# Other PSUM banks and another last quarter product for the seventh product of a two-level Winograd matmul

## The chip, the cores and the metric

The kernel runs on one core of one Trainium2 chip. The time is the device time of one execution in microseconds; the number compared is the median over runs.

## The reference

Two fp32 matrices of 4096 x 4096 are multiplied and a leaky ReLU with slope 0.01 follows.

```python
x = np.matmul(a, b)                       # 4096 x 4096 by 4096 x 4096, fp32
return np.where(x > 0, x, alpha * x)      # alpha = 0.01
```

## The kernel before

**Regions.** The output is cut into sixteen regions of 1024 x 1024: four groups `g` (1024 rows each) by four columns `j`. The first region is done in a plain way; the other fifteen stand in the list `regions`, three of group 0 and then four of each of the groups 1, 2 and 3. Matrices are rounded to fp16 on their way in; products add up in fp32 in the eight PSUM banks (128 x 512 each).

**One region.** A region is one step of the Strassen-Winograd scheme: seven products of 512 x 2048 by 2048 x 512 in place of eight. A product, made by `product` (line 722), is 64 matmuls of 128x128 by 128x512 into four banks. The four banks of one set are called `y`, those of the other `z`; from region to region the sets change places (`ybank`, `zbank`), so the next region's first product writes the four banks that are `z` now, `zbank + 0` first, then `+1`, `+2`, `+3`. Sums of A's blocks (`sum_a`, line 531) and of B's blocks (`b_sum`, line 561) are made on VectorE; results are collected in fp32 tiles `c` by ScalarE copies (`keep`, line 735) and VectorE adds (`add`, line 815). `leave` applies the leaky ReLU (line 307) and stores (line 820).

**Quarters.** In nine regions the scheme is applied a second time to the seventh product, and in six of these (`both`) to the sixth too; the three others are the first regions of the groups 1 to 3. Then the product is seven quarter products (`quarter_product`, line 673) of 16 matmuls of 128x128 by 128x256 each. `into(bank)` lets the result lie in one extra bank; `onto(r, n)` lets it add to what two of the banks `y` hold already. In the names of the code `x[h, k]` are quarters of the A operand, `b[k, n]` quarters of the B operand, `sx(1)` to `sx(4)` the four sums of A quarters, `t(1)`, `t(2)`, `t(4)` the sums of B quarters. The A sums of one group do not change, so they are made once (`sums_of_a`, line 657, in the group's first region), kept in DRAM (line 658) and loaded again in the two later regions by `load_sums` (line 667). `following(n)` inside `sixth_in_quarters` issues the load of sum `n` for the seventh product; the room that it loads into holds a sum of the sixth product, and the load waits until that sum's quarter product is done: sum 4 waits for `sx1 t1`, sum 2 for `sx2 t2`, sum 1 for `sx4 b11`, sum 3 for `sx3 b01`.

**Order.** The order of the work on each engine is written out by hand: every engine executes its instructions in the order of the code. The DMAs of line 667, the stores of line 820 and the loads of `load_s2` (line 692) are issued by one queue (SP) in that order; the loads of B (`fetch_unit`, line 505) by another (POOL).

**Rooms.** Three pools matter: three rooms `a16` (512 KB each, fp16 128 x 2048), three rooms `x` (2 MB each) and the PSUM banks. A room is written again when its last reader is done; a store to DRAM is such a reader. The tile `t` with the name `q` is one room `x` cut into four parts `t[:, 0]` to `t[:, 3]`; it holds the B sums `tq` and one A sum.

**The two places.** In the six regions `sixth_in_quarters` makes its quarter products in the order `x00 b00`, `sx1 t1`, `x01 b10`, `sx2 t2`, `sx4 b11`, `x11 t4`, `sx3 b01`, in the banks `one, other, third, fourth` (`zbank + 0` to `+ 3`); then comes `seventh_in_quarters`, called as

```python
kept_c = seventh_in_quarters(y, new_bank(zbank + 3), new_bank(zbank + 1), tq, sq)
```

Its order is `x01 b10`, `x00 b00`, `sx4 b11`, `x11 t4`, `sx2 t2`, `sx1 t1`, `sx3 b01`. Its bank `one` is taken up by ScalarE copies at lines 798, 802 and 807 (twice, from the last state of `one`), its bank `other` by VectorE adds at lines 804 and 808, where 808 adds to what a copy of line 807 has made. After it the next region begins.

Of the kernel before, what the change touches and what calls it, by code (L numbers as in the profile page):

```python
# [46 lines left out]
def kernel(  # L47
# [40 lines left out]
    x = small_pool.tile([P, 8], FP32, name="x")  # L88
# [99 lines left out]
    def load_b(j, u, c, wide, nt):  # L188
        nc.gpsimd.dma_start(new_b(j, u, nt)[:, c:c + wide, :], b_rows(j, u, c, wide, nt))
# [13 lines left out]
    def new_bank(i):  # L203
        return psum_pool.tile([P, NT], FP32, name="ps", tag=f"ps{i}")
# [88 lines left out]
    for i, (_, h, u, _, _) in enumerate(steps):  # L293
        made = pieces_a(0, h, u, i == 1) if i else []
        more = []
        if u not in seen:
            more = [lambda u=u, c=c, nt=nt: load_b(0, u, c, 2, nt)
                    for c in range(0, KC, 2) for nt in range(2)]
# [47 lines left out]
    both = []  # L346
# [98 lines left out]
    for i in range(1, len(steps)):  # L445
        t, h, u, first, last = steps[i]
# [16 lines left out]
        t, h, u, first, last = steps[i]  # L463
# [161 lines left out]
    def b_quarter(t):  # L625
        return t.rearrange("p (c n) -> p c n", n=HALF)
# [12 lines left out]
    def sums_of_b(y, to, some=(2, 4, 1)):  # L639
        tt = nc.vector.tensor_tensor  # L640
        f = lambda n: b_quarter(to[n])
        if 2 in some:
            tt(f(2), y[0, 1], y[0, 0], ADD)
        if 4 in some:
            tt(f(4), y[1, 0], f(2), SUB)
        if 1 in some:
            tt(f(1), y[1, 1], f(2), SUB)

    def sums_of_a(g, name, room):

        x = {key: q.rearrange("p c m e -> p c (m e)") for key, q in quarters_of_a(g, name).items()}
        made = {}

        def make(n, x0, x1, op):
            made[n] = room(n)
            f = lambda t: made[t].rearrange("p (c m) -> p c m", m=2 * HALF) if isinstance(t, int) else x[t]
            nc.vector.tensor_tensor(f(n), f(x0), f(x1), op)
            nc.sync.dma_start(kept_q[name][n - 1], made[n])

        make(1, (1, 0), (1, 1), ADD)  # L660
        make(2, 1, (0, 0), SUB)
        make(3, (0, 0), (1, 0), SUB)
        make(4, (0, 1), 2, SUB)
# [5 lines left out]
    def quarter_product(xq, yq, to, first=False):  # L669
        for c in range(KC):  # L670
            for m in range(2):
                rows = slice(m * P, (m + 1) * P)
                nc.tensor.matmul(  # L673
                    to[m], xq[:, c // 2, rows, c % 2], yq[:, c, :],
                    start=first and (c, m) == (0, 0), stop=c == KC - 1, skip_group_check=True,
                )

    def into(bank):
        return [bank[:, m * HALF:(m + 1) * HALF] for m in range(2)]

    def pair(bank):
        return bank.rearrange("p (m n) -> p m n", m=2)

    def new_a16(_=None):
        return a16_pool.tile([P, QUARTER], DT, name="q16", tag="a16")
# [18 lines left out]
    for i, (g, j) in enumerate(regions):  # L704
# [7 lines left out]
        zbank = 4 - ybank  # L712
# [25 lines left out]
        def sixth_in_quarters(pairs, banks, v, y, tq, sq):  # L738


            b = quarters_of_b(i, 1, 0)
            x = quarters_of_a(g, "a22")
            one, other, third, fourth = banks
            t = lambda n: b_quarter(tq[n])
            sx = lambda n: a_quarter(sq[n])
            next_t, next_s = {}, {}
            y7 = quarters_of_b(i, 1, 1)

            def more(r, n, t):
                block = pairs[r][:, :, n * HALF:(n + 1) * HALF]  # L750
                nc.vector.tensor_add(block, pair(t), block)

            def following(n, room=None):
                next_s[n] = new_a16() if room is None else room
                load_sums("s4", next_s, (n,))

            quarter_product(x[0, 0], b[0, 0], into(one), True)
            add(v[:2], y[:2])
            more(0, 0, one)
            add(v[2:], y[2:])  # L760
            quarter_product(sx(1), t(1), into(other), True)
            more(1, 1, other)
            following(4)
            next_t[2] = tq[1]
            quarter_product(x[0, 1], b[1, 0], into(fourth), True)
            leave(v, 1, 1)
            quarter_product(sx(2), t(2), into(one))
            following(2)
            more(0, 1, one)
            sums_of_b(y7, next_t, (2,))  # L770
            more(0, 0, fourth)
            quarter_product(sx(4), b[1, 1], into(other))
            following(1, sq[4])
            next_t[4] = tq[2]
            sums_of_b(y7, next_t, (4,))
            more(0, 1, other)
            quarter_product(x[1, 1], t(4), into(third), True)
            next_t[1] = tq[4]
            sums_of_b(y7, next_t, (1,))
            more(1, 0, third)  # L780
            quarter_product(sx(3), b[0, 1], into(one))
            following(3)
            more(1, 0, one)
            more(1, 1, one)
            return next_t, next_s

        def seventh_in_quarters(y, one, other, tq, sq):

            pairs, kept = new_c(side)
            b = quarters_of_b(i, 1, 1)  # L790
            x = quarters_of_a(g, "s4")
            t = lambda n: b_quarter(tq[n])
            sx = lambda n: a_quarter(sq[n])
            block = lambda r, n: pairs[r][:, :, n * HALF:(n + 1) * HALF]
            onto = lambda r, n: [y[2 * r + m][:, n * HALF:(n + 1) * HALF] for m in range(2)]
            quarter_product(x[0, 1], b[1, 0], onto(0, 0))
            quarter_product(x[0, 0], b[0, 0], into(one), True)
            nc.scalar.copy(block(0, 0), pair(one))  # L798
            quarter_product(sx(4), b[1, 1], onto(0, 1))
            quarter_product(x[1, 1], t(4), onto(1, 0))  # L800
            quarter_product(sx(2), t(2), into(one))
            nc.scalar.copy(block(0, 1), pair(one))
            quarter_product(sx(1), t(1), into(other), True)
            nc.vector.tensor_add(block(0, 1), pair(other), block(0, 1))  # L804
            quarter_product(sx(3), b[0, 1], into(one))
            for n in (1, 0):
                nc.scalar.copy(block(1, n), pair(one))
            nc.vector.tensor_add(block(1, 1), pair(other), block(1, 1))  # L808
            for mt in range(MT):
                nc.vector.tensor_add(kept[mt], y[mt], kept[mt])  # L810
            return kept
# [29 lines left out]
        y = [new_bank(ybank + mt) for mt in range(MT)]  # L841
# [4 lines left out]
        first_of_group = i == 0 or regions[i - 1][0] != g  # L846
        in_quarters = g > 0 and not turning and not final
        both = in_quarters and not first_of_group
# [40 lines left out]
            sum_a(g, "s4")  # L889
        if late_ones:  # L890
            late_ones[0].end()
        if first_of_group and g:
            sums_of_a(g, "a22", new_a16)
        if in_quarters:
            t = x_pool.tile([P, 4, QUARTER], DT, name="q", tag="x")
            tq, sq = {2: t[:, 0], 1: t[:, 1], 4: t[:, 2]}, {4: t[:, 3]}
        if both:
            for n in (1, 2, 3):
                sq[n] = new_a16()
            load_sums("a22", sq, (1, 2, 3, 4))  # L900
# [22 lines left out]
        if turning:  # L923
            new_s(g + 1, "s1")
            t = new_s(g + 1, "s2").rearrange("p k c m e -> p (k c m e)").bitcast(BF16)
            a21 = measure(i + 1, 0, 1, 0, t.rearrange("p (n w) -> p n w", n=4))
            a21.begin()
        if both:
            tq, sq = sixth_in_quarters(u2_pairs, [new_bank(zbank + mt) for mt in range(MT)], v, y, tq, sq)
# [26 lines left out]
                sum_a(g + 1, name)  # L956

        if in_quarters:
            kept_c = seventh_in_quarters(y, new_bank(zbank + 3), new_bank(zbank + 1), tq, sq)
            fetch_b(i + 1, [(1, 1)], (1, 0))  # L960
            new_s(g, "s2")
            load_s2(g, 1)
            leave(kept_c, 0, 1)
        else:
            product(6, y, False)
            fetch_b(i + 1, [(1, 1)], ks)
            if final:
                even = nc.values_load(good[0:1, 0:1], min_val=0, max_val=1)
            _, kept_c = new_c(side)

            def store(mt):
                nc.sync.dma_start(place(g, 0, mt, j, 1), kept_c[mt])

            for mt in range(MT):
                nc.scalar.copy(kept_c[mt], y[mt])  # L975
                leaky(kept_c[mt])
                if not (final and mt == MT - 1):
                    store(mt)
# [5 lines left out]
    with inputs.Else():  # L984
        for m in range(M // RM):
            a_blocks = []
            for u in range(KU):
                t = a_pool.tile([P, KC // 2, RM, 2], BF16, name="a", tag=f"a{u // 2 + 1}{m % 2 + 1}")
# [6 lines left out]
            for n in range(N // NT):  # L995
                banks = [new_bank(n % 2 * 4 + mt) for mt in range(MT)]
                cols = slice(n * NT, (n + 1) * NT)
                for u in range(KU):
                    t = b_pool.tile([P, KC, NT], BF16, name="b", tag=f"b{u // 2 + 1}{n % 2 + 1}")
# [8 lines left out]
                for mt in range(MT):  # L1008
                    t = c_pool.tile([P, 2, NT], FP32, name="c", tag=f"c{side}")[:, 0]
# [38 lines left out]
```

## Time and profile before

| | us |
|---|---|
| three runs | 1573.12, 1574.47 (median), 1579.82 |
| the profiled execution, its own time | 1580.19 |
| its span, first to last instruction | 1578.3 |
| TensorE (PE) busy | 1549.3 (98%) |
| VectorE (DVE) busy | 1127.2 (71%) |
| ScalarE (ACT) busy | 373.3 (24%) |
| GpSimd (POOL) busy | 299.6 (19%) |
| mean granted TensorE clock | 0.998 |

Times in the views of the trace count from the span's first instruction. PE is the matmul unit, PEld its weight load; SPq marks an issue of the SP queue. In a row of the timeline the columns are the start, the duration, the engine, line and operation, what it writes and reads, the count, and in brackets the idle time of the engine before it with what ended that. A matmul's duration includes its way through the array, so one row of 16 overlaps the next; the distance between starts is what it costs.

### The profile page before, as it was taken

The numbers are of one execution on the slowest core, as the hardware profiler recorded it, in microseconds if no ns is written. First come the engines' busy times: TensorE is split into PE (matmuls) and PEld (weight loads), VectorE is DVE, ScalarE is ACT, GpSimd is POOL, SyncE is SP. The second block draws the span as 40 slices with busy tenths as digits, with TensorE's granted clock in tenths as the row PEclk, the third lists the DMA queues.
The fourth block names the chain that finished last, engine by engine and source line by source line (L and its number), as shares of the span: only waits on it lengthen the run. The fifth ranks groups of instructions, "written<-read, shape, count | busy, mean of one in ns | idle before, by whom it ended". The sixth has DMA issues, their size and how long they took to land. (4 is left out here: it accounts for less than half of the span.)

```text
span 1578.3 us, 20106 instructions
## 1 busy us (share of the span) xinstructions
PE 1549.3 (98%) x7995; PEld 781.1 (49%) x7995; DVE 1127.2 (71%) x1265; ACT 373.3 (24%) x390; POOL 299.6 (19%) x482
## 2 busy tenths in 40 slices
PE   9999999999999999999999999999999989999997
PEld 4444444444445455474444547456444454745543
DVE  4378758777975776956797686784879779587463
ACT  2201243512111314301211340511122143151230
POOL 5641110244002011123401102012430110201100
PEclk9999999999999999999999999999999999999999
DMA  9999795999739699599976939789995892969902
GB/s 242 183 214 187 154 279 148 193 200 193 273 87 268 153 191 263 128 265 207 194 274 157 266 95 264 179 179 276 190 251 198 187 266 86 261 162 193 260 27 83
DMA packets 206057, 310.76 MB, mean 197 GB/s; under 512 B 18049, under 2 KB 155521, under 8 KB 199042
## 3 DMA queue, kind: packets, MB, share of 16 engines
q0 software_dynamic: 149376, 141.59, 56.2%
q1 hardware_dynamic: 56290, 167.41, 28.6%
q8 instruction: 64, 1.05, 0.3%
q10 hardware_dynamic: 288, 0.39, 0.1%
q14 instruction: 39, 0.32, 0.1%
HBM read 354.42 MB, written 94.37 MB: 284 GB/s over the span
## 5 line engine op out<-in xcount | busy, mean ns | idle before, releaser
L722 PE MATMUL ps<-b,a 128*128 128x512 f16 x3456 | 754.3, 379 | 11.3 <-DVE c L808 10.7
L722 PEld LDWEIGHTS <-a 128*128 128x128 f16 x3456 | 337.3, 98 | 420.0 <-DVE c L808 14.2
L722 PE MATMUL ps<-b,s 128*128 128x512 f16 x2304 | 503.2, 379 | 0.0
L722 PEld LDWEIGHTS <-s 128*128 128x128 f16 x2304 | 225.5, 98 | 271.8
L561 DVE TENSOR_TENSOR b<-b 128x4096 f16<-128x4096 f16 x112 | 252.7, 2288 | 95.2 <-DMA b<-in_b_dram 83.5
L505 POOL DMA_DIRECT2D b<-in_b_dram x184 | 136.3, 746 | 948.2 <-PE ps L722 625.4
L735 ACT COPY c<-ps 128x512 f32<-128x512 f32 x180 | 92.3, 598 | 484.3 <-PE ps L722 422.7
L139 DVE STREAM_TRANSPOSE a<-a 128x512 uint32<-128x512 uint32 (+2 forms) x120 | 126.7, 1102 | 86.1 <-DMA a<-in_a_dram 84.2
L130 POOL DMA_DIRECT2D a<-in_a_dram x252 | 137.4, 552 | 200.3 <-DVE a L139 118.4
L307 DVE SCALAR_TENSOR_TENSOR c<-c 128x512 f32<-128x512 f32 x240 | 149.4, 684 | 12.7 <-ACT c L975 10.0
L815 DVE TENSOR_TENSOR c<-ps,c 128x512 f32<-128x512 f32 x156 | 97.0, 681 | 85.7 <-PE ps L722 59.2
L227 ACT ACTIVATE sq<-b 128x2048 bf16<-128x2048 f16 x64 | 119.2, 1909 | 107.1 <-DVE sq L236 82.7
L279 PE MATMUL ps<-b,a 128*128 128x512 f16 x512 | 113.0, 379 | 2.8 <-DMA b<-in_b_dram 1.4
L227 ACT ACTIVATE sq<-a 128x2048 bf16<-128x2048 f16 x48 | 89.0, 1910 | 88.7 <-DVE sq L236 67.9
L673 PEld LDWEIGHTS <-q 128*128 128x128 f16 x960 | 94.1, 98 | 11.1
L279 PEld LDWEIGHTS <-a 128*128 128x128 f16 x512 | 49.7, 98 | 63.9 <-issue 3.4
L798 ACT COPY c<-ps 128x512 f32<-128x512 f32 x9 | 5.3, 586 | 263.8 <-PE ps L673 263.8
L673 PE MATMUL ps<-b,q 128*128 128x256 f16 x480 | 57.5, 273 | 0.0
L673 PEld LDWEIGHTS <-s 128*128 128x128 f16 x432 | 43.0, 99 | 10.8 <-issue 4.7
L804 DVE TENSOR_TENSOR c<-ps,c 128x512 f32<-128x512 f32 x9 | 6.2, 691 | 58.1 <-issue 49.8
L239 DVE TENSOR_TENSOR sq<-sq 128x2048 bf16<-128x2048 bf16 x27 | 33.1, 1225 | 17.4 <-ACT sq L227 17.4
L673 PE MATMUL ps<-q,q 128*128 128x256 f16 x384 | 45.4, 273 | 0.0
(94 smaller groups left out, 718.0 us busy)
## 6 DMA issues: line engine op xcount, KB each, us to landing
b<-in_b_dram POOLq DMA_DIRECT2D x192, 512.0 KB, 13.5
out_dram<-c SPq DMA_DIRECT2D x240, 256.0 KB, 6.1
a<-in_a_dram POOLq DMA_DIRECT2D x244, 128.0 KB, 5.5
b<-kept SPq DMA_DIRECT2D x24, 1024.0 KB, 8.2
s<-kept_s SPq DMA_DIRECT2D x18, 1024.0 KB, 7.4
q<-kept_qa SPq DMA_DIRECT2D x24, 512.0 KB, 6.8
q<-kept_qs SPq DMA_DIRECT2D x24, 512.0 KB, 8.8
b<-in_b_dram POOLq DMA_DIRECT2D x24, 256.0 KB, 9.3
```

Of the source, the lines that this page charges most:

```text
L130: nc.gpsimd.dma_start(a16[32 * q:32 * q + 32], src.rearrange("(g i) w -> i g w", i=32))
L139: nc.vector.transpose(part.rearrange("p c m e -> p c (m e)").bitcast(U32) .rearrange("p c (g i) -> p g c i", i=32), src[:, :, i * n:(i + 1 ...
L227: nc.scalar.activation(to, self.parts[n], SQUARE)
L239: nc.vector.tensor_add(total, total, self.held[3])
L279: nc.tensor.matmul(ps, a_cols(at[0, h, u], c, mt, (h, u) == (0, 0)), bt[0, u, nt][:, c, :], start=first, stop=last,)
L307: nc.vector.scalar_tensor_tensor(t, t, alpha, t, op0=MULT, op1=MAX if alpha <= 1 else MIN)
L505: nc.gpsimd.dma_start(t[:, c:c + 4, :], b_rows(j, u, c, 4, nt, g > 0))
L561: nc.vector.tensor_tensor(f(to), f(x0), f(x1), op)
L673: nc.tensor.matmul(to[m], xq[:, c // 2, rows, c % 2], yq[:, c, :], start=first and (c, m) == (0, 0), stop=c == KC - 1, skip_group_check=True,)
L722: nc.tensor.matmul(banks[mt], a_cols(t, c, mt, t is first_a), B(half, nt, k)[:, c, :], start=first and (k, c) == todo[0], stop=(k, c) == t ...
L735: nc.scalar.copy(kept[mt], banks[mt])
L815: nc.vector.tensor_add(to, bank, to)
```

## The change

1. `seventh_in_quarters` gets other extra banks: `one` is `zbank + 3` in the six regions as before and `zbank + 0` in the three; `other` is `zbank + 2` in all nine.
2. In `seventh_in_quarters` the quarter product `x11 t4`, which adds to the banks `y[2]` and `y[3]`, moves from the fourth place to the last, behind the copies and adds that empty `one` and `other`.
3. In `sixth_in_quarters` (the six regions) the quarter products `x11 t4` and `sx3 b01` change places, and with them the VectorE work and the load of sum 3 that follow each.
4. In the three first regions the tile `t` is made before the A sums of `a22`; the sums 2, 3 and 4 are written into `t[:, 0]`, `t[:, 1]`, `t[:, 2]` and only sum 1 into a room `a16`. Before, all four went through the three rooms `a16`.

```diff
             more(0, 1, other)
-            quarter_product(x[1, 1], t(4), into(third), True)
-            next_t[1] = tq[4]
-            sums_of_b(y7, next_t, (1,))
-            more(1, 0, third)
             quarter_product(sx(3), b[0, 1], into(one))
             following(3)
             more(1, 0, one)
             more(1, 1, one)
+            quarter_product(x[1, 1], t(4), into(third), True)
+            more(1, 0, third)
+            next_t[1] = tq[4]
+            sums_of_b(y7, next_t, (1,))
             return next_t, next_s
...
             quarter_product(sx(4), b[1, 1], onto(0, 1))
-            quarter_product(x[1, 1], t(4), onto(1, 0))
             quarter_product(sx(2), t(2), into(one))
...
             nc.vector.tensor_add(block(1, 1), pair(other), block(1, 1))
+            quarter_product(x[1, 1], t(4), onto(1, 0))
             for mt in range(MT):
...
-        if first_of_group and g:
-            sums_of_a(g, "a22", new_a16)
         if in_quarters:
             t = x_pool.tile([P, 4, QUARTER], DT, name="q", tag="x")
             tq, sq = {2: t[:, 0], 1: t[:, 1], 4: t[:, 2]}, {4: t[:, 3]}
+        if first_of_group and g:
+            sums_of_a(g, "a22", lambda n: new_a16() if n == 1 else t[:, n - 2])
...
-            kept_c = seventh_in_quarters(y, new_bank(zbank + 3), new_bank(zbank + 1), tq, sq)
+            kept_c = seventh_in_quarters(y, new_bank(zbank + (3 if both else 0)), new_bank(zbank + 2), tq, sq)
```

## The prediction

> **What bounds the kernel now.** I read the page's busy times first, then the waits of PE, then the timeline at each place where PE waited. The page:
>
> ```profile
> PE 1549.3 (98%) x7995; PEld 781.1 (49%) x7995; DVE 1127.2 (71%) x1265; ACT 373.3 (24%) x390; POOL 299.6 (19%) x482
> ```
>
> PE is the bound: of the span of 1578.3 us it is idle for 29.0. An edit that leaves the count of matmuls alone can win only what PE waits, and loses whatever it makes PE wait. The waits of PE (us in total, times, longest) have two rows that touch the change:
>
> ```profile
> PE ps L722 <- DVE c L808: 10.7, 9, 1.2
> PE ps L673 <- DVE c L815: 4.1, 3, 3.8
> ```
>
> The first occurs once in each of the nine quartered regions, at the start of the next region. The timeline around the end of one of them:
>
> ```profile
> 604.43 0.38 PE L722 MATMUL ps<-b,a 128*128 128x512 f16 x1
> 604.63 1.07 ACT L807 COPY c<-ps 128x512 f32<-128x512 f32 x2 [2.91 <-DMA out_dram<-c]
> ...
> 605.25 0.69 DVE L808 TENSOR_TENSOR c<-ps,c 128x512 f32<-128x512 f32 x1 [1.62 <-ACT c L807]
> ...
> 606.00 0.39 PE L722 MATMUL ps<-b,a 128*128 128x512 f16 x1 [1.19 <-DVE c L808]
> ```
>
> At 604.43 the last quarter product is through, the next region gets one matmul into `zbank + 0`, and the second matmul, into `zbank + 1` = `other`, waits 1.19 us for copy and add of lines 807 and 808.
>
> The second row is two waits of under 0.2 us and one of 3.8 us, in the first region of group 3. There VectorE is late, because the A sums share three rooms whose stores must land first (the indented row is what ended line 657's idle time in that region: 7.4 us, four times):
>
> ```profile
> 1241.18 1.22 DVE L657 TENSOR_TENSOR q<-a,a 128x2048 f16<-128x2048 f16 x1
> ...
> 1262.93 2.48 DVE L815 TENSOR_TENSOR c<-ps,c 128x512 f32<-128x512 f32 x4
> ...
> 1267.73 2.48 DVE L815 TENSOR_TENSOR c<-ps,c 128x512 f32<-128x512 f32 x4
> ```
>
> ```profile
>   DMA kept_qa<-q: 7.4, 4
> ```
>
> ```profile
> 1264.58 1.91 PE L673 MATMUL ps<-b,s 128*128 128x256 f16 x16
> 1270.27 3.41 PE L673 MATMUL ps<-b,s 128*128 128x256 f16 x16 [3.78 <-DVE c L815]
> 1273.47 2.12 PE L673 MATMUL ps<-b,q 128*128 128x256 f16 x16
> 1275.42 1.91 PE L673 MATMUL ps<-q,s 128*128 128x256 f16 x16
> ```
>
> ```profile
> 1270.00:1274.00 4.00, 3.73 (x19) 2.70 (x19) 2.62 (x5) 0.29 (x1) 0.00 (x0) 0.57 1.15 285
> ```
>
> The seventh product's second quarter goes into `zbank + 3`, the last bank that the adds at 1267.73 empty. The wait costs more than itself: in the window behind it (the column 0.57 is the granted clock) the two quarters take 3.20 and 1.95 us from start to start, 1.66 us above twice 1.745. Its whole price is 3.78 + 1.66 = 5.4 us. Behind the nine waits of 1.19 us the clock does not fall.
>
> **The banks and the last quarter product.** After the change the region ends with `x11 t4` into `y[2]`, `y[3]`, which the next region does not need for two products. The copy and the add run under it: with `sx3 b01` ending at time E, the rows above put the copy at E + 0.20 to 1.27 and the add at E + 0.82 to 1.51. A quarter product takes 1.745 us from start to start (rows at 683.60 to 687.09 below), so PE comes to the first of these banks at E + 1.74 at the earliest: 0.23 us or more to spare at `other`, 0.47 or more at `one`. So all nine waits go: **-10.7**. In the three first regions `one` is the bank that the adds of line 815 empty first; the 0.3 us of small waits goes too. The two ScalarE copies have 1.74 us of PE work between a product into `one` and the next into it (lines 798 and 802; the first had twice that), against 0.2 us and half of the 1.07 us that two copies take: no wait.
>
> **The A sums of the first regions.** Without the room waits the twelve VectorE steps from 1241.18 (four `a22` sums, four `s4` sums, four of B, 1.2 us each) end near 1255.7. Two waits can remain: the third `s4` sum takes the room of the first `a22` sum, and the B sums take `t[:, 0]` to `t[:, 2]`, whose stores must have landed.
>
> ```profile
> DMA to landing us min/median/max: 4.1/6.8/8.6
> ```
>
> With the longest landing of these stores (8.6), the first wait is 1242.4 + 8.6 against 1248.4 wanted, 2.6 us, and the store issued at 1246.1 lands at 1254.7, before the by then delayed B sum asks. VectorE is then ready by 1258.3 instead of 1262.93; the second adds can follow 4.8 us later, 1263.1, before PE needs them (1264.58 + 0.2). The 3.8 us wait and the slow clock behind it go: **-5.4**.
>
> **What the new order wants earlier.** In the six regions the seventh product now asks for `sx2`, `sx1` and `sx3` one quarter, 1.74 us, earlier; their loads do not start earlier, except that of sum 3, issued behind the moved `sx3 b01`. The slowest of the six:
>
> ```profile
> 683.60 1.91 PE L673 MATMUL ps<-q,a 128*128 128x256 f16 x16
> 685.35 1.91 PE L673 MATMUL ps<-b,q 128*128 128x256 f16 x16
> 687.09 3.66 PE L673 MATMUL ps<-b,s 128*128 128x256 f16 x32
> ...
> 697.57 1.91 PE L673 MATMUL ps<-b,q 128*128 128x256 f16 x16
> ```
>
> ```profile
> L667 SPq DMA_DIRECT2D q<-kept_qs x3: 319/327/632, 682.2 to 687.3; - x3
> ```
>
> ```profile
> DMA to landing us min/median/max: 10.0/11.1/11.5
> ```
>
> The three issues are sums 2, 1 and 3; the last has the shortest time, so sum 3 lands at 687.3 + 10.0 = 697.3, 0.3 us before 697.57 needs it. After the change it is needed at 695.83: **a new wait of 1.5 us**, unless it lands earlier for its earlier issue. The last row of the same view for the other five, in the order of time:
>
> ```profile
> DMA to landing us min/median/max: 9.1/9.9/10.6
> DMA to landing us min/median/max: 8.2/8.9/9.6
> DMA to landing us min/median/max: 8.8/8.8/9.7
> DMA to landing us min/median/max: 9.2/9.9/10.7
> DMA to landing us min/median/max: 8.1/8.4/9.6
> ```
>
> Issue to need was 10.3 us for sum 3 and is 8.5 counted from the old issue. So the waits are 0.6, 1.5, 0, 0.3, 0.7, 0: 3.1 us. Does the earlier issue help? What the queues moved from 688 to 698 us (packets, MB, share of the 16 engines):
>
> ```profile
> q1 hardware_dynamic: 828, 2.20, 61.1%
> q0 software_dynamic: 855, 0.86, 50.6%
> ```
>
> The engines are full, and the SP queue (q1) moves 0.22 MB a us, so that a sum of 0.5 MB comes 2.4 us behind the one before it, whenever it was issued. I take it as not helping: **+3.1**, bounds 2 (sum 3 comes 1.74 us earlier; sum 1, issued 0.2 us behind 683.60 and 11.5 on its way, lands at 695.3 for a need two quarters before 695.83 + 1.74, at 694.08, and then sets 1.2 us, two others under 0.5) and 4.5 (each of six 0.25 later).
>
> The Trainium skill, DMA: Bandwidth & Descriptors, section "Anatomy of one DMA", gives about 2.0 us plus bytes over 436 GB/s; that would be an estimated 3.2 us for 512 KB and no new wait, which would make the sum below 3.1 us less. The trace has that only as its shortest load of these sums:
>
> ```profile
> DMA to landing us min/median/max: 3.2/8.1/11.5
> ```
>
> **Edits with one answer.** The sixth's `sx3 b01` adds to bank `one` 1.74 us earlier, at 683.60 in this region, and the VectorE read of that bank must be over:
>
> ```profile
> 682.05 0.69 DVE L751 TENSOR_TENSOR c<-ps,c 128x512 f32<-128x512 f32 x1 [0.35 <-PE ps L673]
> ```
>
> It is, at 682.74. `t(1)` for the seventh is made behind `x11 t4`: 0.2 us, an add of 0.69 and a sum of 1.2 put it 2.1 us into the seventh, and it is needed four quarters in, at 7.0. `load_s2` (line 692, SP) waits for the room of `q`, now read until the region's end: it issues 1.7 us later; the stores of the seventh behind it in the queue wait for adds that need the same end, and what it loads is read two whole products later. Loads of B on POOL whose room is freed by `b[0, 1]` start 1.74 us earlier. All at 0.
>
> **The sum.** Against the profiled run: 1580.19 - 10.7 - 0.3 - 5.4 + 3.1 = 1566.9. The timed runs are another base: the slowest, 1579.82, stands 5.35 above the median 1574.47, which is the 5.4 of the group 3 wait; so the median run most likely did not have it. Then 1574.47 - 11.0 + 3.1 = 1566.6; from the fastest run, 1573.12, 1565.2. I take 1566.0. A measurement of this kernel can tell about 0.5%, 7.9 us, from no change: the border is 1566.6.
>
> **Rivals.** *The loads are in time*: they land a microsecond or more earlier where nothing is profiled. Then 1574.47 - 11.0 = 1563.5, down to 1562. For it: three of six regions are within 0.3 us of no wait. Against: full DMA engines in all the places.
>
> *The wait at the region's end stays*, because copy, add or the loads come about a microsecond later than reckoned, or the change does not do what it says and some of the nine waits only move to another bank: 1569 to 1577. Against: spares of 0.23 us and more where the events hang on each other with fixed distances, and each engine follows the order of the code.
>
> *The loads of B push the sums back* (slower). The moved `sx3 b01` frees half of a B block 1.74 us earlier, and POOL issues 1 MB of loads (line 505) at 685.8 rather than in the second row here:
>
> ```profile
> 684.06 1.48 POOL L505 DMA_DIRECT2D b<-in_b_dram  x2 [7.26 <-PE ps L673]
> 687.55 1.48 POOL L505 DMA_DIRECT2D b<-in_b_dram  x2 [2.02 <-PE ps L673]
> ```
>
> If these go ahead of the sums, 1 MB at 0.31 MB a us (both queues) is 3.3 us more for each region: waits of 3.9, 4.8, 3.0, 3.6, 4.0 and 2.9, 22.2 in all, and the three longer than 3.78 bring the slow clock, 1.66 each: 1574.5 - 11.0 + 22.2 + 5.0 = 1591. It eats the gain from 1.4 us more per region and shows as slower from 2.8. Against: the POOL queue works in order, and moved only 0.86 MB from 688 to 698, less than the 1 MB of the first row, which is ahead either way. The Trainium skill, DMA: Bandwidth & Descriptors, section "Queues, rings and completion order", has each DMA engine go round the queues packet by packet, and within a queue in ring order; by that q0 takes a share from q1 before and after, and the trace, with both queues moving, agrees.
>
> **How the numbers follow.** New waits of 2 to 4.5 us (1564.2 to 1568.4): 0.62. Loads in time: 0.20. The wait stays or comes back: 0.11. Slower: 0.07. Of the first case some six in ten lie under the border: faster 0.37 + 0.20 = 0.57; same 0.25 + 0.11 = 0.36; slower 0.07. The range, 1562.5 to 1571, leaves out the slower case, most of the case that the wait stays and the lowest end of the second.
>
> **What would show it.** Right: no wait of line 722 for the add behind the seventh; no wait of 3.8 us in group 3 and granted clock 1.00 there; waits of line 673 for `q<-kept_qs` of 0.3 to 1.5 us in about four of the six regions, the one near 695 the longest. Wrong: such waits in all six or above 2 us; a wait of line 722 for a copy or add of the seventh; VectorE still waiting for `kept_qa` near 1250 long enough to delay line 815.

## The result and the profile after

The changed kernel takes 1565.64 us (median of six runs, 1562.75 to 1567.66). Six runs of the kernel before have their median at 1579.09 (1573.12 to 1581.92). The ratio of the runs is 0.9921, 95% interval 0.9898 to 0.9944: the change is faster by about 12.5 us (the medians differ by 13.45). The profiled execution of the changed kernel took 1564.15 us, span 1562.3.

The busy row of the page and the first three rows of the waits of PE (us in total, times, longest) of the changed kernel:

```profile
PE 1547.7 (99%) x7995; PEld 779.9 (50%) x7995; DVE 1126.4 (72%) x1265; ACT 373.5 (24%) x390; POOL 299.7 (19%) x482
```

```profile
PE turned L366 <- DVE a_rounded L350: 1.7, 1, 1.7
PE ps L673 <- DMA q<-kept_qs: 1.7, 5, 0.5
PE ps L279 <- DVE part L318: 1.3, 4, 0.4
```

PE is idle for 14.6 us in place of 29.0. The rows with 10.7 and 4.1 us are gone; a new one, line 673 waiting for the loaded sums, has come. The other two rows belong to the kernel's start and are no part of the change. The rows count waits of 0.15 us and more; smaller ones show only in the distances between starts.

The end of the second quartered region, the place of the first timeline in the prediction (the lines 807 and 808 of before are 806 and 807 now):

```profile
599.94 1.92 PE L673 MATMUL ps<-b,q 128*128 128x256 f16 x16
...
601.70 1.91 PE L673 MATMUL ps<-q,s 128*128 128x256 f16 x16
601.90 1.07 ACT L806 COPY c<-ps 128x512 f32<-128x512 f32 x2 [3.42 <-PE ps L673]
...
602.52 0.69 DVE L807 TENSOR_TENSOR c<-ps,c 128x512 f32<-128x512 f32 x1 [1.87 <-DMA out_dram<-c]
...
603.44 2.75 PE L722 MATMUL ps<-b,a 128*128 128x512 f16 x12
```

Copy and add now run under `x11 t4` (601.70); the add ends at 603.21, 0.23 us before PE starts the next region at 603.44, and the next region's first twelve matmuls run without a gap.

The seventh product of the third quartered region, where the prediction had its longest new wait:

```profile
684.74 3.66 PE L673 MATMUL ps<-b,s 128*128 128x256 f16 x32
688.23 1.91 PE L673 MATMUL ps<-b,q 128*128 128x256 f16 x16
690.64 1.92 PE L673 MATMUL ps<-q,q 128*128 128x256 f16 x16 [0.50 <-DMA q<-kept_qs]
692.93 1.92 PE L673 MATMUL ps<-q 128*128 128x256 f16 x16 [0.38 <-DMA q<-kept_qs]
694.72 1.92 PE L673 MATMUL ps<-b,q 128*128 128x256 f16 x16
696.48 1.91 PE L673 MATMUL ps<-q,s 128*128 128x256 f16 x16
```

```profile
L667 SPq DMA_DIRECT2D q<-kept_qs x3: 319/326/724, 679.8 to 683.2; - x3
```

```profile
DMA to landing us min/median/max: 10.8/11.5/11.5
```

From 688.23 to 690.64 are 2.41 us for a quarter of 1.745, then 2.29 and 1.79: 1.26 us lost over the seventh. The last load is issued 1.56 us before the seventh starts (before: 0.2 us after that start) and takes 11.5 us in place of 10.0.

PE already waits at `sx2 t2` and `sx1 t1`, for the sums 2 and 1, and hardly at `sx3 b01`. Sum 3 sets the total all the same: it lands at 683.19 + 11.5 = 694.7, where it would be wanted, without any wait, at 684.74 + 5 x 1.7465 = 693.47. The waits before it only spend its 1.2 us earlier. So it is in all six regions: of the 4.4 us that they lose together, 2.8 show at the two quarters before, and sum 3 lands 0.3 to 1.2 us later than it would be wanted.

In the first region of group 3 VectorE waits 1.0 and 0.38 us for the stores in place of 7.4, begins the first adds 15.55 us after the first sum, and is idle 3.85 us before the second adds, where PE waited for it before:

```profile
1233.59 1.22 DVE L657 TENSOR_TENSOR q<-a,a 128x2048 f16<-128x2048 f16 x1
...
1241.73 1.23 DVE L657 TENSOR_TENSOR q<-s 128x2048 f16<-128x2048 f16 x1 [1.00 <-DMA kept_qa<-q]
...
1246.86 1.22 DVE L645 TENSOR_TENSOR q<-b,q 128x2048 f16<-128x2048 f16 x1 [0.38 <-DMA kept_qa<-q]
...
1249.14 2.48 DVE L815 TENSOR_TENSOR c<-ps,c 128x512 f32<-128x512 f32 x4
...
1257.87 2.48 DVE L815 TENSOR_TENSOR c<-ps,c 128x512 f32<-128x512 f32 x4 [3.85 <-PE ps L722]
```

Between the two profiled executions, by the starts of the matmuls at the borders of the stretches:

| stretch | us |
|---|---|
| nine region ends, 1.36 each | -12.3 |
| the seventh in the first regions of the groups 1 and 2, 0.34 each | -0.7 |
| the seventh in the first region of group 3 | -5.6 |
| the seventh in the six regions: +1.04, 1.26, 0.52, 0.60, 0.59, 0.38 | +4.4 |
| stretches without an edit (kernel's start, between the groups 1 and 2, behind the last matmul) | -1.9 |
| span, 1578.3 to 1562.3 | -16.0 |

### The profile page after: what moved, and what is told of

It is laid out like the page before. It is cut to its first block, busy times and chain, and to the rows that moved or that the text cites. A ratio compares the mean times of both kernels' runs of the same rounds, so it can differ in the third digit from the quotient of the medians.

```text
span 1562.3 us, 20105 instructions
## 1 busy us (share of the span) xinstructions
PE 1547.7 (99%) x7995; PEld 779.9 (50%) x7995; DVE 1126.4 (72%) x1265; ACT 373.5 (24%) x390; POOL 299.7 (19%) x482
## 5 line engine op out<-in xcount | busy, mean ns | idle before, releaser
L239 DVE TENSOR_TENSOR sq<-sq 128x2048 bf16<-128x2048 bf16 x27 | 33.1, 1226 | 17.1 <-ACT sq L227 17.1
## 6 DMA issues: line engine op xcount, KB each, us to landing
b<-in_b_dram POOLq DMA_DIRECT2D x192, 512.0 KB, 14.6
```

The costliest lines, as they stand in the source:

```text
L239: nc.vector.tensor_add(total, total, self.held[3])
```

## Experiments

Each experiment is an edit of the kernel before or of the changed kernel. "Lost in the seventh" is the distance between its first and last quarter less six times 1.7465 us, from the profiled execution, summed over the six regions; "lost at an end" is the same for the change of regions.

**Only the last quarter product moved**, on the kernel before:

```diff
             quarter_product(sx(4), b[1, 1], onto(0, 1))
-            quarter_product(x[1, 1], t(4), onto(1, 0))
...
             nc.vector.tensor_add(block(1, 1), pair(other), block(1, 1))
+            quarter_product(x[1, 1], t(4), onto(1, 0))
```

> The kernel before with one edit: in the seventh product x11 t4 goes last. Banks, the order of the sixth and the rooms of the A sums stay. Theory (a quarter product behind the copy and the add covers them, whatever the banks): the next region starts 1.36 us earlier at all nine places (start to start; the wait row gave 1.19), also with other = bank 1, which the add leaves free 0.23 us before PE comes to it. The sums 2, 1 and 3 are then wanted 1.74 us earlier, and the six regions wait 3 to 5 us together. Group 3 can still be late in its first region (5.4 to 5.9 us). Net about -8 us against the kernel before. Rival (the other banks did it, the order only helps): the wait at the region's end stays at a good part of 1.2 us, net near 0.

1569.05 us, ratio 0.9936 (0.992 to 0.9953), 9.35 us below the median of the kernel before. Nothing is lost at the nine ends any more (0.00 each, 1.36 before), with the old banks; 4.8 us are lost in the seventh of the six regions. The wait of group 3 is there, 2.9 us, with the slow clock behind it:

```profile
PE ps L673 <- DVE c L815: 3.3, 3, 2.9
PE ps L673 <- DMA q<-kept_qs: 1.9, 2, 1.5
```

So the order of the seventh alone takes the whole wait at the ends and brings the new waits, about as large as in the changed kernel (4.8 and 4.4 us). The rival that the banks did it falls.

**Only the banks**, on the kernel before:

```diff
-            kept_c = seventh_in_quarters(y, new_bank(zbank + 3), new_bank(zbank + 1), tq, sq)
+            kept_c = seventh_in_quarters(y, new_bank(zbank + (3 if both else 0)), new_bank(zbank + 2), tq, sq)
```

> The kernel before with one edit: the extra banks are those of the changed kernel, the order is the old one. Theory: copy and add still come behind the last quarter product, so the waits at the nine ends stay; with other = bank 2 PE gets two matmuls in before it waits in place of one, so the loss is 1.36 - 0.22 = 1.14 us each, start to start; where one is bank 0 (three places) the first matmul waits for both copies, 1.3 us, and the add is nearly hidden behind that. No waits for the loaded sums. Rival (the banks do most of it): under 0.5 us at each end.

One run, 1571.95 us, so its trace is what counts:

```profile
PE ps L722 <- DVE c L808: 5.8, 6, 1.0
PE ps L722 <- ACT c L807: 3.5, 3, 1.2
PE ps L673 <- DVE c L815: 1.8, 1, 1.8
```

The ends lose 1.15 us in six regions and 1.32 in three. The wait in group 3 is down to 1.8 us (the seventh there loses 1.97 in place of 5.60), since the extra product goes to the bank that the late adds empty first, and no slow clock follows. In the first regions of the groups 1 and 2 nothing is lost any more. That is what the banks are worth.

**Only the rooms of the A sums**, on the kernel before (the fourth edit of the change):

> The kernel before with one edit: the A sums 2 to 4 of a22 leave by the parts of the tile q. Theory: VectorE's waits for kept_qa before line 657 fall from 24.7 us to under 6, the wait of 3.8 us in the first region of group 3 and the slow clock behind it are gone; the nine waits of 1.19 us stay. Net -5.4 to -5.9 us against a run of the kernel before that had the wait, 0 against one that did not. Rival (the bank taken for the extra product cured it, not the rooms): the 3.8 us wait stays.

1573.10 us, ratio 0.9965 (0.9951 to 0.9979), 5.3 us below the median of the kernel before. VectorE's waits for the stores are 3.1 us in place of 24.7, and of the wait in group 3 only the 0.2 that the other first regions have too is left:

```profile
PE ps L722 <- DVE c L808: 10.7, 9, 1.2
```

```profile
PE ps L673 <- DVE c L815: 0.5, 3, 0.2
```

The same kernel before was run eight more times beside it, 1575.48 to 1579.77, median 1578.4. The seventh of that region loses 0.34 us here in place of 5.60, which is 5.26 less and as much as the medians differ. That points to the wait being in most of the runs, not in the slowest alone. Only one execution of the kernel before has a trace, but the three experiments that keep the old rooms have VectorE late at that place too (waits of 2.9, 1.8 and, in two parts, 2.4 us).

**The changed kernel with the old rooms**:

```diff
-            sums_of_a(g, "a22", lambda n: new_a16() if n == 1 else t[:, n - 2])
+            sums_of_a(g, "a22", new_a16)
```

(made, as before, ahead of the tile `t`)

> The changed kernel with one edit undone: the A sums of a22 leave by the three rooms a16 again. Theory: VectorE's waits for kept_qa are 25 us again and it is late in the first region of group 3, but the extra bank is now the first that its adds empty, 1.8 us before the last one; so PE waits there some 1 to 2 us in place of 3 to 3.8, and the granted clock does not fall. Time 1 to 3 us above the changed kernel. Rival (only the rooms cure it): 3 us or more of wait and the slow clock, 5 us above the changed kernel.

1567.21 us, beside 1564.69 of the changed kernel on the same chip. The first region of group 3 loses 2.75 us. The granted clock stays at 1.00. Only part of the wait is for VectorE:

```profile
1261.42 1.91 PE L673 MATMUL ps<-b,s 128*128 128x256 f16 x16 [0.96 <-DVE c L815]
1263.16 1.91 PE L673 MATMUL ps<-b,q 128*128 128x256 f16 x16
1266.54 3.65 PE L673 MATMUL ps<-q,q 128*128 128x256 f16 x32 [1.47 <-ACT c L798]
```

The second wait was not foreseen: `sx2 t2` adds to the bank that the copy of line 798 reads. With `x11 t4` moved away only one quarter lies between the two, and here the copy came late. The trace says what held it, a store:

```profile
1258.99 6.94 SPq L820 DMA_DIRECT2D out_dram<-c  x8
```

```profile
1265.91 0.59 ACT L798 COPY c<-ps 128x512 f32<-128x512 f32 x1 [33.38 <-DMA out_dram<-c]
```

The copy writes a tile `c` whose two stores must have landed. VectorE's lateness makes them late: they are the first two of the eight, and the second lands at 1265.8. In the changed kernel the same copy waits only for its product on PE. Banks and rooms thus cure the same wait twice: the rooms take nearly all of it (5.3 of 5.6 us on the kernel before), the banks somewhat over half.

**The changed kernel with the old order of the sixth**:

```diff
+            quarter_product(x[1, 1], t(4), into(third), True)
+            next_t[1] = tq[4]
+            sums_of_b(y7, next_t, (1,))
+            more(1, 0, third)
             quarter_product(sx(3), b[0, 1], into(one))
             following(3)
             more(1, 0, one)
             more(1, 1, one)
-            quarter_product(x[1, 1], t(4), into(third), True)
-            more(1, 0, third)
-            next_t[1] = tq[4]
-            sums_of_b(y7, next_t, (1,))
```

> The changed kernel with one edit undone: the sixth product ends with sx3 b01 again, so the load of sum 3 and the B loads behind it start 1.74 us later. Theory (the DMA engines are full and the SP queue works in order, so sum 3 lands about 2 us behind sum 1 whenever it is issued): sum 3 lands at the same distance from the seventh's start as in the changed kernel (9.1 to 9.9 us), the six regions wait 4.4 us together as there, within 1 us; time equal to the changed kernel. Rival A (a load follows its issue): sum 3 lands 1.7 us later and the six regions wait some 10 us more together. Rival B (the B loads, started earlier, push the sums back): the six regions wait less, 3 us or under.

1565.34 us, ratio 0.9912 (0.9895 to 0.9928): equal to the changed kernel. Lost in the seventh: 6.9 us in this execution, 2.5 more than in the changed kernel's, so the expected "within 1 us" was too narrow; neither rival's figure (10 us more, or 3 us and under) came. The landings tell it better. The view of the loads in the third quartered region, where the seventh starts at 684.92:

```profile
L667 SPq DMA_DIRECT2D q<-kept_qs x3: 320/327/564, 680.0 to 685.1; - x3
```

```profile
DMA to landing us min/median/max: 10.8/11.0/12.4
```

Sum 3, issued at 685.1, lands 11.0 us later at 696.1, 2.0 us behind sum 1 (issued at 681.6, 12.4 us). In the changed kernel sum 3 is issued 1.7 us earlier against the seventh's start and lands at 694.7, again 1.8 us behind sum 1 (681.4 + 11.5 = 692.9). In these two executions and the one of the kernel before, sum 3 lands 1.8 to 2.2 us behind sum 1 in all eighteen places, with the issues 1.75 or about 3.5 us apart (2.9 in one). Issuing it earlier only makes it wait longer in the queue.

**The changed kernel without the loads** of the seventh's sums in the six regions:

```diff
             def following(n, room=None):
-                next_s[n] = new_a16() if room is None else room
-                load_sums("s4", next_s, (n,))
+                next_s[n] = sq[n]
```

> The changed kernel without the 24 loads of the seventh's A sums in the six regions: the seventh multiplies the sixth's A sums instead. Theory: each quartered end of the six regions runs at 1.745 us a quarter without any wait, 4.4 us less than the changed kernel, 1561.2 from its 1565.6. Rival (something else, the ScalarE copies or the weight loads, makes the new waits): the waits of the fourth to sixth quarter of the seventh stay.

1557.89 us, ratio 0.9865 (0.9849 to 0.9882). Nothing is lost in any seventh (0.00 in each region), and no wait of line 673 is in the list. So the loads are the new waits, all of them, and not the ScalarE copies, which run as before. The time is 7.7 us under 1565.64 (7.5 under the experiment before, on the same chip) where 4.4 had been expected. Of the difference between the two profiled spans, 5.7 us, 4.4 are the waits, 0.7 lies ahead of all that was changed and 0.6 between the groups 1 and 2. The profiled execution of the changed kernel is one of its faster ones, 1.5 us below its median. Where the rest of the 7.7 lies is not settled.

**Two of the sums made, not loaded**, on the changed kernel:

```diff
-            following(1, sq[4])
+            next_s[1] = sq[4]
...
-            following(3)
+            next_s[3] = new_a16()
...
+            if both:
+                f = lambda q: q.rearrange("p c m e -> p c (m e)")
+                for n, x0, x1, op in ((1, x[1, 0], x[1, 1], ADD), (3, x[0, 0], x[1, 0], SUB)):
+                    nc.vector.tensor_tensor(sq[n].rearrange("p (c m) -> p c m", m=2 * HALF), f(x0), f(x1), op)
             quarter_product(x[0, 1], b[1, 0], onto(0, 0))
```

> The changed kernel, but in the six regions sums 1 and 3 of the seventh's A operand are made anew by VectorE (two operations of 1.2 us, behind the stores' leaky ReLU) in place of two loads of 512 KB; sums 4 and 2 are still loaded. Theory (the new waits are loads in a full queue): VectorE has them ready some 7 us into the seventh, before they are wanted at 7.0 and 8.7; only sum 2 can be late, by up to 0.7 us; the six regions wait 1 to 2 us together in place of 4.4, time 2.5 to 3.5 us below the changed kernel. Rival (VectorE is too busy there: it was busy 9.6 of the 10 us around the seventh's start): the sums come late, the waits are 4 us or more again, with VectorE as what ended them.

1559.31 us, ratio 0.9877 (0.9862 to 0.9892): faster than both kernels, 5.4 us below the changed kernel on the same chip (more than the 2.5 to 3.5 expected; the six regions lose 3.7 us less than in the second profile of the changed kernel, shown next, and where the rest lies is not settled). In the third quartered region the seventh starts at 683.67 and VectorE makes the two sums here:

```profile
688.04 2.35 DVE L799 TENSOR_TENSOR q<-s 128x2048 f16<-128x2048 f16 x2
```

They are there 6.7 us into the seventh, wanted at 7.0 and 8.7. The six regions lose 1.55 us, in two of them, both times at `sx2 t2`, waiting for sum 2, one of the two that are still loaded:

```profile
PE ps L673 <- DMA q<-kept_qs: 1.2, 2, 0.6
```

**The changed kernel again**, beside the last ones:

> The changed kernel once more, for a comparison on one chip with the others of this call and for a second profile. Theory: no wait at the nine ends, waits for the loaded sums of 3.5 to 5.5 us over the six regions, no late VectorE in group 3; 11 to 14 us below the kernel before.

1564.69 us, ratio 0.9909 (0.9896 to 0.9923). Nothing lost at the ends; 5.2 us lost in the six regions, of which 3.1 in one:

```profile
690.97 1.92 PE L673 MATMUL ps<-q,q 128*128 128x256 f16 x16 [2.73 <-DMA q<-kept_qs]
```

That region lost 1.26 us in the first profile of the same kernel. How late a load lands there differs from run to run by more than the waits that I reckoned with.

## Why the prediction was right, point by point

**The nine ends.** The mechanism was right, and the order is its whole cause. The size was off: I took the idle time of the row, 1.19 us, and the loss is 1.36. From the rows of before, 604.43 to 606.00 are 1.57 us for one matmul that takes about 0.21 from start to start. The row counts idle time only behind the modelled end of the matmul before (0.38 us after its start), and so misses some 0.17 us in every wait. Nine losses of 1.36 are -12.3 in place of -10.7. The same holds for the small waits, 0.34 each in place of under 0.2.

**Group 3.** -5.4 forecast, -5.6 measured; the difference is the same 0.17. VectorE was to be ready 14.5 to 17.1 us behind the first sum; it took 15.55. The slow clock behind the wait was rightly counted in.

**The loads.** The forecast was 3.1 us, between 2 and 4.5; 4.4 and 5.2 were measured in two executions, and the second is outside. The mechanism was right: the time at which sum 3 lands, less the time at which it is wanted, sets what each region loses, though the waits begin at the sums 2 and 1. The longest loss is where it was forecast. The step "an earlier issue of sum 3 does not help" held: the distance to sum 1 stayed at about 2 us with the issue 1.7 us earlier or later.

The size was not right, and both signs that the prediction named as wrong for it came: by the distance of starts all six regions lost in the first profile, where I had four, and the second has a wait above 2 us, 2.73. I took the landings of one execution as fixed. In the two regions for which I had no wait, the third and the last, sum 3 landed 8.4 and 8.3 us after the seventh's start in the profile that I read; in the two experiments that keep the old order of the seventh it landed there after 9.1 and 9.3, and after 8.5 and 9.1. The same reckoning from those two executions would have given 2.6 and 4.1 us in place of 3.1.

**The base.** This step was wrong. From three runs I concluded that the median run most likely did not have the wait of group 3. Of the 23 timed runs of the kernel before that are on record, only the two fastest of those three are below 1575.4; the later medians are 1578.4 and 1578.6, and taking that wait away alone brought 5.3 us against the first of these. The two may have lacked the wait, which no trace of them can show, but they were not typical. The right base was the profiled run. The gain against the median shown, 8.5 us, was too small for this reason; 12.5 was measured.

The forecast time hardly hangs on this: a run that never had the wait and a run that is freed of it come to the same, 1566.6 from the one and 1566.9 from the other. With the terms as measured (-12.3 - 0.7 - 5.6 + 4.4) it is 1566.0 from the profiled run. That the forecast, 1566.0, met 1565.64 so closely is in part luck: what is won was put 2.2 us too low and what is lost 1.3 us too low, and stretches that no edit touches differ by 1.9 us between the two profiled executions.

**The rivals.** The loads were not in time: leaving them out brings 7.7 us in timed runs. The wait at the ends did not stay or move to another bank, with 0.23 us to spare. The B loads that start earlier did not push the sums back: with them started late again the waits were not shorter.

**The page's rule.** The estimate from the Trainium skill (DMA: Bandwidth & Descriptors, "Anatomy of one DMA"), 3.2 us for a load of 512 KB, does not hold in this place: the loads took 10.8 to 11.5 us in the third quartered region, in a queue with stores and other loads ahead of them. That section is about DMAs of the gpsimd path, and these loads are issued on SP.

## What to carry to other kernels

Where a stage ends in a PSUM bank that the next stage writes at once, put a product that goes elsewhere behind it: here that covered copy and add completely, where other banks alone left 1.15 to 1.32 of 1.36 us. Before moving work forward, list every operand that it or its neighbours need earlier, and look at when each lands; a load behind others in a full queue was not helped here by an earlier issue (whether fewer bytes ahead of it would help was not tested), and making the operand anew on an engine with time left can be cheaper than the load. The price of a wait is the distance between starts, not the idle time that a row shows, and one profiled landing is a sample.

## What the runs showed of the hardware

- Two waits of PE, 3.78 and 2.94 us by their rows, went with 3.4 us at half the granted clock. Here is the second, in the kernel where only the last quarter product moved, with the granted clock around its end (the column 0.57) and then in finer steps (the columns 1.00, 0.52 and 0.50):

```profile
1264.70 3.42 PE L673 MATMUL ps<-b,s 128*128 128x256 f16 x16 [2.94 <-DVE c L815]
```

```profile
1264.00:1268.00 4.00, 3.30 (x17) 2.30 (x17) 3.05 (x6) 0.00 (x0) 0.00 (x0) 0.57 1.14 285
```

```profile
1264.00:1264.40 0.40, 0.00 (x0) 1.00 1.14 277
1264.40:1264.70 0.30, 0.00 (x0) 0.52 1.10 283
1264.70:1267.80 3.10, 3.10 (x15) 0.50 1.14 285
```

  The wait of 2.73 us in the changed kernel's second profile had no such end, the clock stayed at 1.00:

```profile
690.00:700.00 10.00, 9.01 (x73) 7.05 (x74) 3.46 (x6) 1.66 (x3) 2.59 (x5) 1.00 1.18 254
```

  The Trainium skill, TensorE: Matmul & The Clock Gate, section "Why this matters for your kernels", asks for no idle gaps over about 3 us between bursts of matmuls. The trace agrees as far as three waits can: with the 0.17 us that a row misses, the two gaps are 3.94 and 3.11 us and the one without a slow clock is 2.90. The length alone does not tell when the clock falls. In the first wait it was still 1.00 when PE went on, 3.78 us after the row's idle time began, and fell 0.2 us later; in the second it fell 0.3 us before PE went on, 2.65 us after the idle time began.

- Sum 3 landed 1.8 to 2.2 us behind sum 1 in 46 of the 48 places of the eight profiles that have both loads, with the DMA engines full (61 and 51% of their time for the two queues in the window that the prediction shows), whether it was issued 1.5 to 1.75 or 2.9 to 3.5 us behind it. The two other places are in the experiment with the banks alone, 2.8 and 3.4 us with issues 3.5 us apart. In the second of them both loads landed 8.6 to 8.7 us after their issue, so the distance of the issues did count there.

- Before these loads, sum 4 is issued when the SP queue is empty and the POOL queue keeps the DMA engines busy. In all six places of the kernel before it then moves no packet for 3.45 to 3.53 us. Here is the third quartered region, with the load issued at 678.55; all that moves in the 3.4 us behind it is POOL's (packets, MB, share of the 16 engines):

```profile
q0 software_dynamic: 660, 0.66, 119.8%
```

  The two queues move side by side, as in the prediction's window from 688 to 698, only after that. With POOL's queue idle, a load of line 667 issued at 1332.07 moved its first packet after 0.95 us and landed after 3.2 us.
